# Rotary embedding, interleaved pairs: tables on a second queue, wider VectorE steps, and an early first store

## The chip, the cores and the metric

The kernel runs on one core of a Trainium2 chip. The metric is the device time of one execution in microseconds (us). "The ring" is the queue of DMA descriptors that GpSimd fills; "SP" and "ACT" are the queues of the Sync and Activation engines (the Activation engine is also called ScalarE); "DVE" is VectorE. A packet is one piece of a transfer, as the trace records it, moved by one of the 16 DMA engines. A bubble is a stretch in which these engines have no packet to move, and slack is time that nothing waits for. The profiled span is about 1.8 us shorter than the time of the run it belongs to.

## The reference

```python
x: (8, 2048, 16, 64) float32;  cos, sin: (2048, 32) float32
x1, x2 = x[..., 0::2], x[..., 1::2]        # as pairs
out1 = x1 * cos - x2 * sin
out2 = x1 * sin + x2 * cos                 # interleaved again, float32
```

x is 67.1 MB and the output as much, the tables 0.5 MB together. Three VectorE operations on each element, 134.7 MB through the DMA engines: a kernel of this kind is about moving data.

## The kernel before

128 partitions hold 16 positions of a batch each. A batch is one 8.4 MB load, converted to bf16 on the way, and one 8.4 MB store, converted back to float32. Five batch buffers are in SBUF; all DMAs that convert are issued by GpSimd, in program order, so they stand in one ring.

```python
KP = 4; NX = 5; HEAD = 2; TAIL = 4              # positions per VectorE step, buffers, ...
def load(b, k0=0):  nc.gpsimd.dma_start(out=tiles[b][:, k0:], in_=x_t[b, :, k0:])  # its buffer: cut
def store(b, k1=K): nc.gpsimd.dma_start(out=out_t[b, :, :k1], in_=tiles[b][:, :k1])
def rotate(b, k0, k1):       # ... three tensor_tensor: qt = x*s_tab; x *= c_tab; x += swap(qt)

for k in range(HEAD):                            # first 1 MB of x, as float32, two pieces
    nc.sync.dma_start(out=head[:, k : k + 1], in_=x_t[0, :, k : k + 1])
nc.sync.dma_start(out=cos_sb, in_=cos_t)
nc.sync.dma_start(out=sin_sb, in_=sin_t)
load(0, HEAD)
for b in range(1, NX):
    load(b)
# ... ScalarE converts the head, VectorE builds c_tab and s_tab from cos_sb and sin_sb ...
for b in range(B):
    if b == 0:
        rotate(b, 0, HEAD)
        rotate(b, HEAD, KP)
    for k0 in range(KP if b == 0 else 0, K, KP):
        rotate(b, k0, k0 + KP)
    if b < B - 1:
        store(b)
    if b >= 1 and b - 1 + NX < B:
        load(b - 1 + NX)                         # waits for store b - 1: same buffer
store(B - 1, K - TAIL)                           # 6 MB; the last 2 MB go out on SP, from ScalarE
# ...
```

## Time and profile before

| | before |
|---|---|
| time, median of the first 3 runs | 317.64 us (317.61 to 317.65) |
| profiled span | 316.0 us |
| VectorE busy | 221.8 us, 70% |
| bytes through HBM | 134.7 MB, 426 GB/s over the span |
| first VectorE instruction | 44.22 us |

These lines of the page of the kernel before give the busy time of VectorE, its busy tenths and those of the DMA engines in 40 slices of 7.9 us, what each DMA queue took of the 16 engines' time, and the HBM traffic.

```profile
DVE 221.8 (70%) x102; ACT 6.9 (2%) x4; POOL 8.9 (3%) x20
DVE  0000039999999999999999999999999999100000
DMA  9899999999999999999999999999999999999996
q0 software_dynamic: 2304, 98.04, 96.8%
q1 hardware_dynamic: 720, 3.67, 3.1%
HBM read 67.63 MB, written 67.11 MB: 426 GB/s over the span
```

The line of nines under "DMA": from the first slice to the last but one the DMA engines have no room. VectorE has five empty slices in front and five at the end. The chain of waits does not help in this kernel: 91% of it is "another core or an unknown queue", that is, transfers in the ring that it can't take apart. So read the rate in windows. Columns: window, length, busy time and instructions of VectorE, ScalarE and GpSimd, granted clock, DMA share, GB/s as counted on the destination's side.

```profile
90.00:100.00 10.00, 9.83 (x6) 0.00 (x0) 0.00 (x0) 1.00 1.00 210
110.00:120.00 10.00, 9.86 (x5) 0.00 (x0) 0.00 (x0) 1.00 0.98 419
```

The first window holds loads alone, counted as 2-byte elements (210 GB/s, so 420 of float32 read from HBM). The second holds stores alone: 419. It is one rate, counted on the float32 side. The start in the timeline of the kernel before (start, duration, engine, line, operation, what ended the idle time):

```profile
0.74 0.85 SPq L85 DMA_DIRECT2D st<-in_x_dram  x2
1.24 2.80 POOL L56 DMA_DIRECT2D xt<-in_x_dram  x5 [0.80 <-PEq L144]
2.11 0.43 SPq L87 DMA_DIRECT2D sin_sb<-in_sin_dram  x1
44.22 0.45 DVE L94 CAST s_tab<-sin_sb 128x512 bf16<-128x512 f32 x1 [44.22 <-DMA sin_sb<-in_sin_dram]
74.53 0.54 POOL L59 DMA_DIRECT2D out_dram<-xt  x1 [70.48 <-DVE xt L80]
```

VectorE waits 44 us for a table of 256 KB that was asked for at 2.1 us, and the first store is issued at 74.5 us.

### The profile page before, as it was taken

The numbers are of one execution on the slowest core, as the hardware profiler recorded it, in microseconds if no ns is written. First come the engines' busy times: TensorE is split into PE (matmuls) and PEld (weight loads), VectorE is DVE, ScalarE is ACT, GpSimd is POOL, SyncE is SP. The second block draws the span as 40 slices with busy tenths as digits, with TensorE's granted clock in tenths as the row PEclk, the third lists the DMA queues.
The fourth block names the chain that finished last, engine by engine and source line by source line (L and its number), as shares of the span: only waits on it lengthen the run. The fifth ranks groups of instructions, "written<-read, shape, count | busy, mean of one in ns | idle before, by whom it ended". The sixth has DMA issues, their size and how long they took to land.

```text
span 316.0 us, 198 instructions
## 1 busy us (share of the span) xinstructions
DVE 221.8 (70%) x102; ACT 6.9 (2%) x4; POOL 8.9 (3%) x20
## 2 busy tenths in 40 slices
DVE  0000039999999999999999999999999999100000
ACT  1200000000000000000000000000000000000400
POOL 3000000000000000000000000000000000000000
DMA  9899999999999999999999999999999999999996
GB/s 241 198 257 212 212 207 236 228 199 199 253 212 265 398 498 431 398 332 261 203 399 465 328 203 199 481 448 265 199 307 423 398 440 481 406 398 481 417 431 263
DMA packets 3025, 101.72 MB, mean 322 GB/s; under 512 B 336, under 2 KB 336, under 8 KB 848
## 3 DMA queue, kind: packets, MB, share of 16 engines
q0 software_dynamic: 2304, 98.04, 96.8%
q1 hardware_dynamic: 720, 3.67, 3.1%
q14 instruction: 1, 0.01, 0.0%
HBM read 67.63 MB, written 67.11 MB: 426 GB/s over the span
## 4 chain that ended last, share of the span: by engine, by line
another core or an unknown queue 91%; DMA 2%; ACTq 1%; ACT 1%; SPq 0%; issue 0%
DMA st<-in_x_dram 2%; ACTq L144 1%; ACT xt L92 1%; ACT L92 0%; SPq L85 0%; ACT xt L116 0%; ACTq L116 0%; ACTq L92 0%
## 5 line engine op out<-in xcount | busy, mean ns | idle before, releaser
L75 DVE TENSOR_TENSOR xt<-xt,c_tab 128x4096 bf16<-128x4096 bf16 (+1 forms) x33 | 73.5, 2228 | 1.1
L80 DVE TENSOR_TENSOR xt<-xt,qt 128x4096 bf16<-128x4096 bf16 (+1 forms) x33 | 73.5, 2228 | 1.1
L74 DVE TENSOR_TENSOR qt<-xt,s_tab 128x4096 bf16<-128x4096 bf16 (+1 forms) x33 | 73.5, 2228 | 1.1
L94 DVE CAST s_tab<-sin_sb 128x512 bf16<-128x512 f32 x1 | 0.5, 453 | 44.2 <-DMA sin_sb<-in_sin_dram 44.2
L59 POOL DMA_DIRECT2D out_dram<-xt x8 | 4.3, 535 | 202.1 <-DVE xt L80 202.1
L116 ACT COPY xt<-xt 1x1 bf16<-1x1 bf16 x1 | 0.2, 193 | 286.3 <-DMA out_dram<-xt 286.3
L56 POOL DMA_DIRECT2D xt<-in_x_dram x8 | 4.4, 561 | 52.1 <-DMA out_dram<-xt 51.3
L117 ACT CAST st<-xt 128x4096 f32<-128x4096 bf16 x1 | 3.6, 3599 | 0.0
L92 ACT CAST xt<-st 128x2048 bf16<-128x2048 f32 x1 | 1.9, 1899 | 0.0
L92 ACT ACT_TABLE_LOAD x1 | 1.3, 1283 | 6.4 <-DMA st<-in_x_dram 6.4
L96 DVE CAST c_tab<-cos_sb 128x1024 bf16<-128x1024 f32 x1 | 0.7, 684 | 0.0
L95 DVE TENSOR_SCALAR s_tab<-sin_sb 128x512 bf16<-128x512 f32 x1 | 0.4, 443 | 0.0
L133 POOL MEMSET const-float32-0.0<- 128x1 f32 x1 | 0.1, 99 | 0.2 <-issue 0.2
L133 POOL MEMSET const-bfloat16-1.0<- 128x1 bf16 x1 | 0.1, 102 | 0.0
L133 POOL MEMSET const-float32-1.0<- 128x1 f32 x1 | 0.1, 99 | 0.0
L133 POOL MEMSET const-uint8-127<- 128x1 uint8 x1 | 0.1, 99 | 0.0
## 6 DMA issues: line engine op xcount, KB each, us to landing
xt<-in_x_dram POOLq DMA_DIRECT2D x7, 4096.0 KB, 58.0
out_dram<-xt POOLq DMA_DIRECT2D x1, 6144.0 KB, 49.4
xt<-in_x_dram POOLq DMA_DIRECT2D x1, 3584.0 KB, 22.7
out_dram<-st SPq DMA_DIRECT2D x1, 2048.0 KB, 15.5
st<-in_x_dram SPq DMA_DIRECT2D x2, 512.0 KB, 4.5
cos_sb<-in_cos_dram SPq DMA_DIRECT2D x1, 256.0 KB, 22.4
sin_sb<-in_sin_dram SPq DMA_DIRECT2D x1, 256.0 KB, 42.1
out_dram<-xt POOLq DMA_DIRECT2D x7, 54.0
```

Source lines behind the costliest of these rows:

```text
L56: nc.gpsimd.dma_start(out=tiles[b][:, k0:], in_=x_t[b, :, k0:])
L59: nc.gpsimd.dma_start(out=out_t[b, :, :k1], in_=tiles[b][:, :k1])
L74: nc.vector.tensor_tensor(out=rows(qt[:, :nk]), in0=rows(xp), in1=tab(s_tab), op=mult)
L75: nc.vector.tensor_tensor(out=rows(xp), in0=rows(xp), in1=tab(c_tab), op=mult)
L80: nc.vector.tensor_tensor(out=x3, in0=x3, in1=q_swap, op=add)
L92: nc.scalar.copy(out=tiles[0][:, :HEAD], in_=head[:, :HEAD])
L94: nc.vector.tensor_copy(out=s2[:, :, 0], in_=sin_sb)
L95: nc.vector.tensor_scalar_mul(s2[:, :, 1], sin_sb, -1.0)
L96: nc.vector.tensor_copy(out=c_tab.rearrange("p k (i j) -> p (k i) j", j=2), in_=cos_sb.to_broadcast([P, K * D2, 2]),)
L117: nc.scalar.copy(out=tail, in_=tiles[B - 1][:, K - TAIL :])
L133: nc = _bacc.Bacc("TRN2", target_bir_lowering=False, num_devices=1)
L144: with _tile.TileContext(nc) as tc:
```

## The change

Its intent: get the tables early, so that VectorE starts early; use fewer and longer VectorE instructions; and let the first stores start while loads are still under way.

```diff
-    KP = 4
+    KP = 8
...
-    def store(b, k1=K):
-        nc.gpsimd.dma_start(out=out_t[b, :, :k1], in_=tiles[b][:, :k1])
+    def store(b, k0=0, k1=K):
+        nc.gpsimd.dma_start(out=out_t[b, :, k0:k1], in_=tiles[b][:, k0:k1])
...
-        nc.sync.dma_start(out=cos_sb, in_=cos_t)
-        nc.sync.dma_start(out=sin_sb, in_=sin_t)
+        nc.scalar.dma_start(out=cos_sb, in_=cos_t)
+        nc.scalar.dma_start(out=sin_sb, in_=sin_t)
         load(0, HEAD)
-        for b in range(1, NX):
-            load(b)
+        load(1)
...
                 rotate(b, 0, HEAD)
+                store(b, 0, HEAD)
+                for c in range(2, NX):
+                    load(c)
                 rotate(b, HEAD, KP)
...
-                store(b)
+                store(b, HEAD if b == 0 else 0)
...
-        store(B - 1, K - TAIL)
+        store(B - 1, 0, K - TAIL)
```

## The prediction

> **What bounds it now.** The 16 DMA engines. The slice view shows DMA at 9 tenths or more in nearly every slice, the queue table 96.8% + 3.1%, while DVE is busy 221.8 us of 316.0. Narrow windows show one rate for every kind of traffic: pure loads, 90 to 100 us, 210 GB/s counted on the bf16 side, so 420 in HBM; pure stores, 110 to 120 us, 419. In the semaphore records the 8 MB transfers land every 19.3 us: loads 44.0, 63.3, 82.6, 102.2; stores 121.5, 140.8; load 160.9; store 180.0; the end 257.1, 276.5, 295.8, and the last 8 MB at 315.1. That is 434 GB/s, without a bubble and without visible gain where a store follows a load. All 134.7 MB at this pace are 310.0 us. Only about 6 us are not streaming: first packet near 1.8 us, engines full from about 2.7 us, the first 1 MB in 4 KB packets a little slow [...], about 1 us after the last landing.
>
> **What the change does.**
> 1. cos and sin leave the queue where each of their 2 KB packets waits for a 28 or 32 KB packet of x; they land at 24.1 and 44.2 us today. The Trainium skill, "DMA: Bandwidth & Descriptors", "Queues, rings and completion order", says each engine takes turns between rings by packet, and the packet counts agree (32 of x to 32 of the tables in 5 us). On a ring that starts before the x loads they should land at 4 to 8 us. DVE then starts near 7 us. But by "Issuing engines are not separate DMA queues" on that page the bytes use the same 16 engines, which are full from 2.7 us. Gain: what the second ring fills of the ramp between 1.8 and 2.7 us, 0 to 0.6 us.
> 2. By 8 positions: from 1.23 us (2048) and 2.29 us (4096) I estimate 4.43 us (8192). DVE falls to about 214 us; off the path, worth 0.
> 3. The first 1 MB stored after the second load: GpSimd waits for the first rotation (12 to 16 us) before it issues loads 2 to 4. The ring holds loads 0 and 1 until about 43 us, so no bubble. 2.4 us of store move forward, none are added; 8 KB packets may cost 0.1 to 0.2 us more than 64 KB ones. Load 5 still waits for all of store 0 (about 121 us), with store 1 behind it in the ring; the later order is unchanged.
>
> **On the critical path:** nothing but the ramp. The 30 us by which DVE comes earlier turn into slack. I predict 317.3 us, range 316.6 to 318.0; chance of faster by over 2% 0.01, within 2% 0.98, slower by over 2% 0.01.
>
> **What would show it.** Right: DVE's first wait ends before 10 us; the first store is issued near 15 us, loads 2 to 4 right behind; landings still 19.3 us apart; DMA share about 1 in every window; load 1 lands within 1 us of 44.0 (the same bytes); the page's HBM rate stays 424 to 428 GB/s. Wrong on 1: load 1 lands at 42 us or before. Wrong on 3: a window after 40 us with a DMA share well below 1, or the small store and the load behind it taking more than 21.9 us together.
>
> **What would make it wrong.** A better rate where a short store stands among loads (a load reads 4 bytes and writes 2, a store the reverse, so overlap could pay; the 19.3 us at today's borders speak against it). GpSimd waiting far longer for the first rotation. Slower issue of loads while DVE is busy.

## The result

The changed kernel takes 317.88 us (317.80 to 318.05, 6 runs) against 317.61 us (317.43 to 317.65, 6 runs) of the kernel before in the same rounds. Ratios here are the mean time of one kernel's fast runs over that of the other's of the same rounds, so not quite the ratio of the medians; this one is 1.0011, with a 95% interval of 0.9998 to 1.0024. No difference of any size, and if there is one, it is a loss of some 0.3 us. The result was correct in every run.

The same lines of the page, changed kernel:

```profile
DVE 214.3 (68%) x54; ACT 6.9 (2%) x4; POOL 9.4 (3%) x21
DVE  0049999999999999999769970799508994000000
DMA  7999999999999999999999999999999999999996
q0 software_dynamic: 2448, 98.04, 96.9%
q1 hardware_dynamic: 432, 3.15, 2.6%
q10 hardware_dynamic: 288, 0.52, 0.5%
HBM read 67.63 MB, written 67.11 MB: 426 GB/s over the span
```

VectorE has 7.5 us less to do, starts three slices earlier, and now shows gaps in the middle, where it waits for loads. The line of the DMA engines is as before, and so are the bytes and the rate. Windows of the changed kernel around the early store, and one of stores alone:

```profile
40.00:45.00 5.00, 4.96 (x2) 0.00 (x0) 0.00 (x0) 1.00 0.92 234
45.00:50.00 5.00, 4.96 (x2) 0.00 (x0) 0.54 (x1) 1.00 1.19 290
130.00:140.00 10.00, 9.93 (x3) 0.00 (x0) 0.00 (x0) 1.00 1.04 433
```

A packet counts in the window in which it starts, so single windows read a little under or over 1; 0.92 and 1.19 together are 1.06 for 10 us. There is no bubble. The start in the timeline:

```profile
0.73 0.39 ACTq L86 DMA_DIRECT2D cos_sb<-in_cos_dram  x1
1.16 0.47 ACTq L87 DMA_DIRECT2D sin_sb<-in_sin_dram  x1
18.36 1.28 ACT L91 ACT_TABLE_LOAD   x1 [18.36 <-DMA st<-in_x_dram]
20.07 0.46 DVE L93 CAST s_tab<-sin_sb 128x512 bf16<-128x512 f32 x1 [20.07 <-DMA sin_sb<-in_sin_dram]
25.91 0.54 POOL L59 DMA_DIRECT2D out_dram<-xt  x1 [23.46 <-DVE xt L80]
26.44 1.59 POOL L56 DMA_DIRECT2D xt<-in_x_dram  x3
```

VectorE starts at 20.07 us instead of 44.22, and the first store is issued at 25.91 instead of 74.53. The times at which transfers landed (the last of the 16 completion increments of each, from the trace's semaphore records, us from the span's start) show what became of that. e4 and e9 are experiments told of below: the changed kernel without the small store, and with the small store after load 4.

```
                    before   after      e4      e9
x piece 1 (SP)         4.7     5.9     5.9     5.8
cos                   24.1     6.1     6.0     6.0
x piece 2 (SP)         6.3    18.3    16.2    16.1
sin                   44.2    20.0    20.0    20.5
load 0                23.9    24.8    24.8    24.7
load 1                44.0    44.6    44.1    44.0
store 0, first 1 MB      -    47.1       -   104.9
load 2                63.3    66.4    63.4    63.4
load 3                82.6    85.7    82.7    82.7
load 4               102.2   105.0   102.4   102.4
store 0 complete     121.5   122.0   121.7   121.8
store 1              140.8   141.3   141.1   141.1
...
store 6              295.8   296.0   295.7   295.7
store 7, last 2 MB   315.1   315.3   315.1   315.0
```

From load 1 to store 6 there are 13 times 8.4 MB in both kernels (the small store is a part of store 0): 251.7 us before, 251.4 after, 19.4 and 19.3 us each. The early store moved 2.4 us of work forward, and every landing from load 2 to load 4 came about 3 us later for it. At "store 0 complete" the two kernels have moved the same bytes again, and are 0.5 us apart; at the end, 0.2 us.

### The profile page after: what moved, and what is told of

Same layout as the page of the kernel before. It is cut to its first block, busy times and chain, and to the rows that moved or that the text cites. A ratio compares the mean times of both kernels' runs of the same rounds, so it can differ in the third digit from the quotient of the medians.

```text
span 316.2 us, 153 instructions
## 1 busy us (share of the span) xinstructions
DVE 214.3 (68%) x54; ACT 6.9 (2%) x4; POOL 9.4 (3%) x21
## 4 chain that ended last, share of the span: by engine, by line
another core or an unknown queue 87%; DMA 5%; ACTq 1%; ACT 1%; SPq 0%; issue 0%
DMA st<-in_x_dram 5%; ACTq L147 1%; ACT xt L91 1%; ACT L91 0%; SPq L85 0%; ACT xt L119 0%; ACTq L119 0%; ACTq L91 0%
## 5 line engine op out<-in xcount | busy, mean ns | idle before, releaser
L74 DVE TENSOR_TENSOR qt<-xt,s_tab 128x8192 bf16<-128x8192 bf16 (+2 forms) x17 | 71.0, 4174 | 29.2 <-DMA xt<-in_x_dram 28.6
L80 DVE TENSOR_TENSOR xt<-xt,qt 128x8192 bf16<-128x8192 bf16 (+2 forms) x17 | 71.0, 4175 | 0.6
L75 DVE TENSOR_TENSOR xt<-xt,c_tab 128x8192 bf16<-128x8192 bf16 (+2 forms) x17 | 71.0, 4174 | 0.6
```

The source lines that it names most:

```text
L74: nc.vector.tensor_tensor(out=rows(qt[:, :nk]), in0=rows(xp), in1=tab(s_tab), op=mult)
L75: nc.vector.tensor_tensor(out=rows(xp), in0=rows(xp), in1=tab(c_tab), op=mult)
L80: nc.vector.tensor_tensor(out=x3, in0=x3, in1=q_swap, op=add)
```

## The experiments

**The theory:** the 16 DMA engines are saturated by bytes from about 3 us on. Earlier VectorE work, shorter VectorE work and another order of the transfers turn into slack. **The rivals:** (C) VectorE or the chain load, rotation, store does cost time, and parts of the change cancel each other; (O) loads and stores that stand side by side overlap, so their order matters; (M) the limit is the HBM and not the engines. Eleven kernels were run; all but two compute the right result, and those two say so.

### The parts alone: e1, e2, e4

e1 is the kernel before with the tables on ACT, e2 the kernel before with `KP = 8`, e4 the changed kernel without the early store.

```diff
# e1                                              # e2
-        nc.sync.dma_start(out=cos_sb, ...)       -    KP = 4
-        nc.sync.dma_start(out=sin_sb, ...)       +    KP = 8
+        nc.scalar.dma_start(out=cos_sb, ...)
+        nc.scalar.dma_start(out=sin_sb, ...)
# e4, against the changed kernel
-        load(1)
+        for b in range(1, NX):
+            load(b)
-                store(b, 0, HEAD)
-                for c in range(2, NX):
-                    load(c)
-                store(b, HEAD if b == 0 else 0)
+                store(b)
```

> The kernel before with cos and sin on the Activation queue, nothing else. Theory A (the 16 DMA engines are saturated by bytes; the 0.27 us that the changed kernel lost comes from sharing the start between two hardware rings, since its first x piece landed at 6.1 instead of 4.7 us): 317.7 to 318.0, like the changed kernel; sin lands near 20 us. Theory B (the 0.27 us comes from the small store in the ring): 317.6 as before. Theory C (DVE's late start cost time and another part of the change gave the gain back): clearly below 317.4.

> The kernel before with VectorE by 8 positions, nothing else. Theories A and B: 317.6 as before within 0.1 us, although DVE's busy time falls by about 7.5 us to 214 us. Theory C (VectorE is on the path): faster by more than 1 us.

> The changed kernel without the early store (all five loads issued at once, store 0 in one piece). Theory A (start): 317.8 to 318.0, as the changed kernel. Theory B (small store): 317.6, as before. If the early store is a hidden gain (better mix of loads and stores): slower than the changed kernel, over 318.2.

Measured, with the kernel before at 317.46 us (317.36 to 317.83) in the same rounds: e1 317.60 us (317.34 to 317.71; ratio 1.0003, 0.9990 to 1.0015), e2 317.58 us (317.51 to 317.72; 1.0004, 0.9992 to 1.0017), e4 317.50 us (317.47 to 317.70; 1.0002, 0.9988 to 1.0015). So no part gains anything that another gives back: rival C falls for all three. In e2 VectorE had 214.2 us to do in place of 221.8, and the time did not move. (In what I expected of e1, the 6.1 us is the landing of cos; the x piece landed at 5.9.) The small loss of the changed kernel is not in the start (theory A), since e1 and e4 share that start and don't show it. It goes with the small store (theory B).

### The early store without the early tables: e3

```diff
# e3, against the changed kernel
-    KP = 8
+    KP = 4
-        nc.scalar.dma_start(out=cos_sb, in_=cos_t)     # and sin
+        nc.sync.dma_start(out=cos_sb, in_=cos_t)       # and sin
```

> The changed kernel with cos and sin back on the Sync queue and VectorE by 4: the early store alone. sin lands near 44 us again, so GpSimd can't issue the store and the loads 2 to 4 before about 49.5 us, while the ring runs dry near 43 us. Theory A/B (the ring must never run dry; the parts of the change hang together): a window near 44 to 52 us with a DMA share far below 1, and 323 to 328 us. Rival (the DMA engines have slack to make up later): 317.6 to 319.

Measured: 327.12 us (326.74 to 327.39; before 317.46; ratio 1.0304, 1.0289 to 1.0318). The timeline of e3 and its windows:

```profile
44.12 0.46 DVE L93 CAST s_tab<-sin_sb 128x512 bf16<-128x512 f32 x1 [44.12 <-DMA sin_sb<-in_sin_dram]
49.71 0.54 POOL L59 DMA_DIRECT2D out_dram<-xt  x1 [47.25 <-DVE xt L80]
50.23 1.60 POOL L56 DMA_DIRECT2D xt<-in_x_dram  x3
```

```profile
43.00:44.00 1.00, 0.00 (x0) 0.00 (x0) 0.00 (x0) 1.00 0.06 16
44.00:45.00 1.00, 0.88 (x3) 0.00 (x0) 0.00 (x0) 1.00 0.00 0
45.00:50.00 5.00, 4.90 (x5) 0.00 (x0) 0.29 (x1) 1.00 0.00 0
```

GpSimd issues in order. With the tables late, it stands at the store until 49.71 us, with loads 2 to 4 behind it, and the engines have nothing left from 43.6 us (the last packet of load 1 ended at 43.5, the last of sin at 43.6) to 50.8 us, when the first of the store began. Those 7.2 us are not made up later; the rest of the 9.7 us is not as clear (after the bubble the 16 engines landed their shares of one large transfer 1.5 to 2.4 us apart up to store 6, in the changed kernel 1.0 to 1.2 us; and load 4 landed 20.9 us after load 3, against 19.6 us in the kernel before). So the parts of the change hang together: the early tables are what makes the early store harmless. In the changed kernel the store is issued at 25.91 us, 17 us before the ring would run dry.

### Is the new slack real? e5, e6

```diff
# e5 from the kernel before, e6 from the changed kernel
         nc.vector.tensor_tensor(out=rows(qt[:, :nk]), in0=rows(xp), in1=tab(s_tab), op=mult)
+        if k0 >= K // 2:
+            nc.vector.tensor_tensor(out=rows(qt[:, :nk]), in0=rows(xp), in1=tab(s_tab), op=mult)
```

> The kernel before with one third-part of VectorE work done twice (the multiplication by sin repeated for positions 8 to 15 of every batch, same result): about 4.65 us more per batch, 37 us in all. Saturated-ring theory: DVE starts at 45.5 us without slack to spare at the end, its last rotation moves from 269 to about 307 us, the ring runs dry at about 296 us and the end moves out: 327 to 332 us. Rival (DVE is on the path everywhere, as much as the DMA): 317.6 + 37 = 355.

> The changed kernel with the same VectorE work done twice (about 4.46 us more per batch, 36 us in all). Saturated-ring theory: DVE starts at 20 us, is done with batch 7 at about 273 us, before the ring runs dry at 296: 317.9 as without it, so the change has bought real slack, 30 us and more, that the kernel does not need. Rival (the earlier start is not usable slack): 327 or more, like the kernel before with this work.

Measured, with the kernel before at 317.49 us: e6 317.89 us (317.82 to 317.96; ratio 1.0012, 0.9997 to 1.0026), the time of the changed kernel to 0.01 us, with some 35 us more VectorE work (249.6 us busy in place of 214.3). e5 321.10 us (321.09 to 321.12; ratio 1.0113, 1.0098 to 1.0128). The direction is as expected, the size is not: 3.6 us, and I had said 10 to 15. In the profile of e6 VectorE started at about 24 us, because sin landed at 23.9 there and not at 20.0; even so the last large store was issued 19 us before the ring ran dry (the first packet of that store began at 294.6):

```profile
275.80 0.53 POOL L59 DMA_DIRECT2D out_dram<-xt  x1 [30.69 <-DVE xt L82]
```

Timeline and windows of e5 at the end:

```profile
297.49 0.53 POOL L59 DMA_DIRECT2D out_dram<-xt  x1 [22.73 <-DVE xt L82]
306.64 3.60 ACT L119 CAST st<-xt 128x4096 f32<-128x4096 bf16 x1
```

```profile
294.00:296.00 2.00, 1.97 (x2) 0.00 (x0) 0.00 (x0) 1.00 0.02 0
296.00:298.00 2.00, 1.97 (x2) 0.00 (x0) 0.51 (x1) 1.00 0.00 0
298.00:300.00 2.00, 1.97 (x2) 0.00 (x0) 0.02 (x1) 1.00 0.91 393
```

I had counted from the last rotation, which ends at 306.5 us as I said. But the last large store covers positions 0 to 11 only and needs just the rotation before it: it is issued at 297.49 us. The ring is empty from 295.1 to 298.6 us, 3.5 us, and that is the whole loss; the last rotation and its conversion hide behind the 6 MB that are then under way. So the change did buy slack: this extra work costs 3.6 us before and nothing after. The kernel as it stands does not need it.

### Does a finer mix of loads and stores pay? e7

```diff
# e7, against the changed kernel (load has a k1 as well)
-            if b < B - 1:
+            if 2 <= b <= 4:
+                for k0 in range(0, K, 4):
+                    load(b - 2 + NX, k0, k0 + 4)
+                    store(b, k0, k0 + 4)
+            elif b < B - 1:
                 store(b, HEAD if b == 0 else 0)
-            if b >= 1 and b - 1 + NX < B:
-                load(b - 1 + NX)
```

> The changed kernel with loads 5, 6, 7 and stores 2, 3, 4 in pieces of 4 positions (2 MB), one load piece, one store piece, in turn. Saturated-engine theory (each packet holds its engine for its wider side, whatever stands next to it): 317.9 to 320. Overlap theory (a load reads 4 bytes and writes 2, a store the reverse, so neighbours overlap and a finer mix pays): up to 48 MB of traffic gain; below 316, and landings of a 2 MB + 2 MB pair well under 9.65 us.

Measured: 318.99 us (318.83 to 319.30; before 317.49; ratio 1.0047, 1.0032 to 1.0062), 1.1 us more than the changed kernel. Over the mixed stretch, stores land at 151.3, 161.0, 170.8, 180.5, 190.2, 199.9, 209.7: one pair of 2.1 MB in and 2.1 MB out every 9.7 us, where two quarters of 19.3 us would be 9.65. Rival O falls: a load and a store that stand side by side take the sum of their times, at this grain at least.

### Less to move, and the same to move without HBM: e8, e10

e8 loads half of the last batch only (VectorE writes zeros in its place; wrong result). e10 takes the last batch's load from a float32 tile in SBUF (wrong result): the same widths, no HBM traffic.

```diff
# e8, against the changed kernel (load has a k1 here too)
-                load(b - 1 + NX)
+                load(b - 1 + NX, 0, K // 2 if b - 1 + NX == B - 1 else K)
+            if b == B - 1:
+                nc.vector.memset(tiles[b][:, K // 2 :], 0.0)
# e10, against the changed kernel, for batch 7 in place of load(7)
+                    tiles[B - 1] = xpool.tile([P, K, HD], bf16, name="xt")
+                    for k in range(0, K, HEAD):
+                        nc.gpsimd.dma_start(out=tiles[B - 1][:, k : k + HEAD], in_=head[:, :HEAD])
```

> Wrong result on purpose: the changed kernel loads only positions 0 to 7 of the last batch (4.2 MB of HBM reads less; VectorE writes zeros instead, a few us of work). Saturated-ring theory: 9.65 us less, 308.2. Rival (the time is set by a chain of waits, load to rotation to store, not by bytes): above 314.

> Wrong result on purpose: the changed kernel, with the load of the last batch taken from a float32 tile in SBUF in place of HBM: eight transfers of 1 MB read, 0.5 MB written, the same widths as the load, but no HBM traffic for 8.4 MB. Theory E (the limit is what the DMA engines move on the wider side): the eight take about 19.3 us together, 318 us. Theory M (the limit is the HBM): they take well under 19.3 us, and the time is below 314.

e8: 308.32 us (308.16 to 308.37; before 317.49; ratio 0.9708, 0.9692 to 0.9725), 9.56 us less than the changed kernel where half of 19.3 us is 9.65. Bytes are time here, one for one, and the end of a chain of waits would not have moved like this.

e10: 318.02 us (318.02 to 318.16; before 317.46; ratio 1.0018, 1.0004 to 1.0032). The page of e10 shows that the HBM traffic has fallen by 8.4 MB:

```profile
HBM read 59.24 MB, written 67.11 MB: 399 GB/s over the span
```

Yet its eight transfers of 1 MB landed between 218.5 (store 3, in front of them) and 238.2 us: 19.6 us, 2.45 each, against 19.3 us for the one load from HBM (218.6 to 237.9 in the changed kernel). Rival M falls for the loads. One thing e10 alone leaves open: its float32 side is read from SBUF, so a limit of SBUF at nearly the same rate would look alike. But the float32 side lay in HBM for the loads, in SBUF for e10, and in HBM again, now written, for the stores, and the rate on that side was 434, 428 and 434 GB/s. The simplest reading is that the DMA engines are full, which is also what their busy share says; a path that all three share was not told apart from them. Whether stores are held by the engines or by the HBM was not tried apart.

### Where the 0.3 us may come from, and a try at the start: e9, e11

```diff
# e9, against the changed kernel: the small store after loads 2 to 4
-                store(b, 0, HEAD)
                 for c in range(2, NX):
                     load(c)
+                store(b, 0, HEAD)
# e11, against the kernel before, with KP = 8: the head of x in one transfer
-        for k in range(HEAD):
-            nc.sync.dma_start(out=head[:, k : k + 1], in_=x_t[0, :, k : k + 1])
+        nc.sync.dma_start(out=head[:, :HEAD], in_=x_t[0, :, :HEAD])
```

> The changed kernel with the 1 MB store still a transfer of its own, but issued after loads 2 to 4, so that it stands in front of the rest of store 0. Open: why the changed kernel is about 0.3 us slower than itself without the small store (e4, 317.5). Theory P (its 8 KB packets and one transfer more cost it, wherever it stands): 317.8. Theory Q (its place costs it: two more borders between loads and stores): 317.5.

> The kernel before with VectorE by 8 and the first 1 MB of x in one transfer of 8 KB packets in place of two of 4 KB ones. An attempt on the ramp, the one place where the engines are not full. Saturated-ring theory: at most 0.3 us to be had, 317.2 to 317.5. If the ramp is longer than I read it: under 317.

e9: 317.67 us (317.47 to 317.85; before 317.46; ratio 1.0007, 0.9994 to 1.0019), between the two theories and within the noise of both. The kernels with the small store among the loads (changed, e6) have medians of 317.88 and 317.89, those without it (e1, e2, e4) 317.50 to 317.60, so the store very likely costs 0.3 us; which part is its packets and which its place stays open. e11: 317.75 us (317.61 to 318.01; ratio 1.0011, 0.9997 to 1.0024): no gain. Its first 8 KB packets did fill the engines by 2.5 us, but sin then landed at 33.5 us and the end did not move. The landings show where the gain went: against e2, which differs from e11 in the head alone, load 3 landed 1.0 us earlier (81.7 against 82.8), but load 4 only 0.2 us earlier (101.9 against 102.2), and the lead stayed that small or smaller. The last load packets ahead of the first store took 2.92 to 3.72 us in e11, 2.43 to 2.71 in e2. So, in these two profiled runs, a microsecond won at the start was mostly lost where the first store follows the loads; no run here settles why. No experiment pointed to a version that beats both kernels.

## Why the prediction was right, and where it was not

- **What bounds the kernel: right.** e8 and e10 show it directly, and 13 large transfers take 251.7 and 251.4 us in the two kernels.
- **The time: right**, 317.88 us against 317.3 foretold, in the range of 316.6 to 318.0 but near its upper end. The sign of the small term was not: I allowed 0 to 0.6 us of gain for the start and 0.1 to 0.2 us of loss for the small store. The start gained nothing (e1, e4), and the loss goes with the store, at about 0.3 us.
- **The early tables: the step failed, without a consequence.** I said that cos and sin would land at 4 to 8 us, that VectorE would start near 7 us, and the first store be issued near 15. sin landed at 20.0, VectorE started at 20.07, the store was issued at 25.91. cos did land at 6.1 us. What I left out is that 1.57 MB (head and tables) do not fit between the first packet at 1.7 us and the first x packet from GpSimd's ring at 5.7 us: 1.07 MB of it had moved by then. The engines were not full before about 3 us, and small packets are slower than large ones (in the kernel before, with the engines full, 171 packets of 4 KB began between 3 and 5 us, which is 350 GB/s). From then on a small packet waits for a turn behind a 28 KB packet that holds its engine 2.13 us. By 7.0 us, 189 of the 256 table packets had ended; the last ended at 17.6 us, and the 4-byte packet that follows the data on each engine took another turn, the last one to 19.7. The second piece of x, which had landed at 6.3 us before, was held up in the same way, to 18.3. The same turns explain the kernel before: a table is 128 packets of 2 KB, 8 on each engine, and so is a load, 8 packets on each engine. cos therefore landed with load 0 (24.1 and 23.9 us) and sin with load 1 (44.2 and 44.0).
- **Why that error cost nothing:** the ring holds load 1 until about 43.5 us (in the changed kernel the first packet of the small store began at 43.3). The store needs to be issued before that; 25.91 is early enough. e3 shows the other side of that edge: at 49.71 us it costs 9.7 us. This was margin, not luck: the prediction gave the ring until about 43 us, and named a far longer wait for the first rotation as what would make it wrong.
- **VectorE by 8: right.** A step of 128x8192 took 4.43 us, as estimated, and VectorE's busy time fell from 221.8 to 214.3 us; e2 shows that it is worth nothing.
- **No bubble, unchanged order: right.** The small store and load 2 behind it landed 21.8 us after load 1 (44.6 to 66.4), just under the 21.9 I gave as a limit.
- **No gain from mixing: right**, by the argument that today's borders show none; e7 shows it for 12 pairs.
- **The 30 us of slack:** VectorE's earlier start became waits for loads in the middle of the kernel. e6 uses up that slack and costs nothing.

The Trainium skill carried two of the steps. "DMA: Bandwidth & Descriptors", "Issuing engines are not separate DMA queues", says that a second issuing engine saves only issue time; e1 agrees, 317.60 against 317.46 us. "Queues, rings and completion order" on that page says that each engine takes turns between rings by packet; the landings of the tables agree, and the mistake was not to count the turns.

## What to carry to other kernels

Before you bring work forward, ask what is waiting for it: where the DMA share is full from the start to the end, an earlier start of another engine becomes slack, and what changed the time here was fewer bytes (e8) or a bubble (e3, e5); e11 shows that a microsecond won at the start need not reach the end. A wait put in front of queued loads on an in-order queue is free only as long as the queue holds work for longer than the wait, so put the two times next to each other (here 25.9 and 43.3 us, and 49.7 and 43.5 in the version that lost 9.7 us). A small transfer that shares the engines with large packets needs as many turns as it has packets on an engine; to have it early, it must be through before the large packets begin.

## What the Trainium skill lacked or had wrong

- "DMA: Bandwidth & Descriptors", "Where 436 GB/s comes from", derives 435 GB/s from the SBUF ports and says that for transfers between HBM and SBUF the HBM side, about 358, binds. For a kernel on one core that sentence is wrong: this one moved 426 GB/s of HBM traffic over the whole span. The same page, "Measured", has it right: it gives 425 GB/s for 16 MB by one core and keeps 358 for both cores of a pair. What the page lacks is that with a conversion on the way the wider side counts: about 434 GB/s held on the float32 side while the loads brought only half as many bytes to SBUF, and nearly so when the source was SBUF as well (e10: 2.45 us for 1 MB to 0.5 MB).
- The same page, "Queues, rings and completion order", tells of turns by packet but not of what a turn costs with packets as large as these. Here the packets of the converting loads were 28 or 32 KB (destination side) and held an engine 2.13 or 2.43 us, those of the stores 64 KB and 2.45 us; 256 KB of sin took until 44.2 us.
- The same page, "Specifications", gives first-byte latencies of about 1 us for GpSimd's DMAs and about 0.6 us for those of SP and ACT. On an empty ring the first took 1.1 us in e3 (49.71 to 50.82) and in e5 (297.49 to 298.59), which agrees; but at the start of the kernel before it took 3.9 us (1.24 to 5.14), and SP's first packet came 1.0 us after its issue (0.74 to 1.74).
- No page has this: the last load packet on each engine ahead of the kernel's first store took 2.65 to 3.02 us in the changed kernel (median 2.93), 2.51 to 3.05 in the kernel before (2.74) and 2.92 to 3.72 in e11 (3.34), where the median of all load packets of this size is 2.43. No run here settles why.
